# A two-layer mixer kernel on one Trainium2 core: how x is loaded at the start, and where the two filter networks stand

## The chip, the cores and the metric

The kernel runs on one core of one Trainium2 chip. The core has five engines with a queue of instructions each: TensorE (PE) for matmuls, VectorE (DVE), ScalarE (ACT), GpSimd (POOL) and SyncE (SP), which here only starts DMA transfers. Each engine takes its instructions in the order in which they were laid out when the program was built, and waits on semaphores for what it needs. The metric is the device time of one execution in microseconds (us); the median of several runs is the result.

## The reference, cut to what matters

x (512 tokens, 1024 wide) and a context (256 tokens) go through two layers. In each layer a modulation row is computed from c, the normalised x is projected by w_in, and three mixers (differential attention, grouped attention, and a long convolution named hyena) make y, which w_out projects. The convolution's filter comes from a small network of three sine layers, once for length 512 and, in the first layer, once for length 256:

```python
def _hyena_filter(L, w1, b1, w2, b2, w3, b3, w4, freq):
    ...
    h = jnp.sin(fr * (z @ w1.astype(f32) + b1.astype(f32)))
    h = jnp.sin(fr * (h @ w2.astype(f32) + b2.astype(f32)))
    h = jnp.sin(fr * (h @ w3.astype(f32) + b3.astype(f32)))
    h = h @ w4.astype(f32)
    ...
def reference(...):
    for l in range(DEPTH):
        shift, scale, gate = jnp.split(jax.nn.silu(c) @ ada_w[l] + ada_b[l], 3, axis=-1)
        h = _rms(x, norm_g[l]) * (1.0 + scale[:, None]) + shift[:, None]
        hc = _rms(xc, norm_g[l]) * (1.0 + scale_c) + shift_c
        qa, ka, va, ga, qg, kg, vg, gg, uh, gh = _prep(h @ w_in[l], gq_q_g[l], gq_k_g[l])
        ...
        filt = _hyena_filter(L, hy_w1[l], ...)
        y = _mixer_output(...)
        if update_ctx:
            filt_c = _hyena_filter(Lc, hy_w1[l], ...)
            ...
        x = x + gate[:, None] * y
    return _rms(x, final_g)
```

## The kernel before, in words

All products are made in three passes: a float32 value is split into a high part (wh, uh, made by a cast on ACT, L152) and the rest (wl, ul, a subtraction on DVE, L156), and `mm3` issues high x high (L138), high x low (L139) and low x high (L140). A weight tile raw [128, 1024] comes in by a DMA on SP (L528) and is split into wh and wl; eight such buffers go round.

The program begins with `startup_loads`. SP loads c, x in four tiles, and between these the small constants: the networks' inputs and weights, identity, columns. An x tile holds 256 of the 1024 columns of all 512 tokens, so that each row read is 1 KB. `x0_rms` sums the squares on ACT, in pieces of 256 columns (L497), and `rsqrt_cols` makes the inverse root r with Ln and Exp on ACT (L168, L169) and a Newton step on DVE (L171 to L175). `scale_x` multiplies x by r on ACT and DVE (L510, L512).

Then follows a loop over four quarters of the width. In each, `mod_quarter` multiplies the modulation weights (adaw tiles, DMA at L357) with silu(c) in 32 small matmuls (psm, L365), adds the bias (mrow, L368), transposes (pst, L370) and writes the columns mA and mB (L372, L373). `make_hT_x` transposes two chunks of x on PE (L467), applies mA and mB on ACT (hf, L469) and splits the result on DVE (hT, L457 and L458). `start_proj` then gives these two chunks to the first two hyena projections (xv of b = 0 and 1, 96 matmuls of 128x512 in all over the four quarters). Next the context is done in the same way (cq, L481, L486; 96 matmuls of 128x256). The results are filtered by a short convolution (cv, L684 to L687) and multiplied on POOL (ux, uc, L707).

The two networks are `filter_mlp`. For each of the three layers PE makes one product (L217 for the first, L219 after it), DVE computes the argument and reduces it to the sine's range in six operations (v and m, L222 to L228), and ACT takes the sine (hmlp, L231). The network for 512 has tiles of 128x512, that for 256 of 64x256; both write their products into the PSUM tile S0. The sine needs another table of functions on ACT than the rest of the kernel; the set in use is changed by an ACT_TABLE_LOAD. In the kernel before, the first network is written ahead of the loop over the quarters and the second within its first turn. A table load (guard) in the second turn brings back the set that holds Exp, and the context's load and all that is written later is kept behind guard by `tc.issue_after`.

`mlp_stack` splits the networks' outputs (hst). `filter_gen` then multiplies them by the last weights (psh, L280 and L281), applies the decay on DVE (fw L284, bw L288), forms the sum s on POOL (L299) and the difference on DVE (L300), sums squares (q on ACT, accf on POOL, L294), splits s and the difference (uh, ul), and transforms them by products with tables (EOf, L308 to L310). PSUM tiles come from small pools: S has two buffers (S0 and S1 at the start, later EOf), pj two, T and O one each. After the filter's transform the next projections (xg) begin.

A scheduler decides, when the program is built, in what order the instructions stand in each engine's queue; it goes by the written order, by its own estimate of times, and by the pools.

Of the kernel before, what the change touches and what calls it, by code (L numbers as in the profile page):

```python
# [10 lines left out]
F32 = mybir.dt.float32  # L11
F32R = mybir.dt.float32r
AF = mybir.ActivationFunctionType
# [55 lines left out]
def hybrid_mixer(ctx: ExitStack, tc: tile.TileContext, a, out):  # L69
# [94 lines left out]
    def rsqrt_cols(ms, n, scale, pool=None):  # L164
        m = small(n, pool)
        DVE.tensor_scalar(out=m, in0=ms, scalar1=scale, scalar2=EPS, op0=ALU.mult, op1=ALU.add)
        r = small(n, pool)
        ACT.activation(r, m, AF.Ln)  # L168
        last_exp[0] = ACT.activation(r, r, AF.Exp, scale=-0.5)  # L169
        t = small(n, pool)  # L170
        DVE.tensor_tensor(out=t, in0=r, in1=r, op=ALU.mult)  # L171
        DVE.tensor_tensor(out=t, in0=t, in1=m, op=ALU.mult)
        DVE.tensor_scalar(out=t, in0=t, scalar1=-0.5, scalar2=1.5, op0=ALU.mult, op1=ALU.add)
        r2 = small(n, pool)
        DVE.tensor_tensor(out=r2, in0=r, in1=t, op=ALU.mult)  # L175
        return r2
# [14 lines left out]
    def startup_loads(xd):  # L191
        zt = [up.tile([33, n], F32, tag="u", name="zt") for n in (512, 256)]
        ws = [ta.tile([128, 64] if i else [33, 2, 64], F32, tag="ta", name="wf") for i in range(3)]
        bc = cp.tile([128, 4], F32, tag="bc", name="bc")
        ct = sw.tile([128, 16], F32, tag="sw", name="ct")
        few = [[(ct, a["cT"]), (zt[0], a["z512"]), (ws[0], a["hy_w1"])], [(bc, a["hy_b"]), (ws[1], a["hy_w2"])],
               [(zt[1], a["z256"]), (ws[2], a["hy_w3"])], [(ident, a["ident"]), (cols[0], a["cols"][0])]]
        xq = []
        for q in range(4):
            t = pa.tile([128, 4, 256], F32, tag="pa", name="xq")  # L200
            SP.dma_start(t, xd[:, q * 256:(q + 1) * 256].rearrange("(t p) n -> p t n", p=128))
            xq.append(t)
            for dst, src in few[q]:
                SP.dma_start(dst, src)
        return ct, xq, (zt, ws, bc)
# [255 lines left out]
    def make_hT_x(xblk, A, B, ks, pools):  # L461
        res = []
        for k in ks:
            pool, tag = pools[k % len(pools)]
            ps = pool.tile([128, 512], F32, tag=tag, name="pst")
            for t in range(4):
                PE.transpose(ps[:, t * 128:(t + 1) * 128], xblk(k, t), ident)  # L467
            h = tp.tile([128, 512], F32, tag="tp", name="hf")
            ACT.activation(h, ps, AF.Identity, bias=B[:, k, 0:1], scale=A[:, k, 0:1])  # L469
            res.append(split2(h, [512]))  # L470
        return res
# [19 lines left out]
    def row_sums(s, t, n):  # L491
        r = small(t)
        DVE.tensor_reduce(out=r, in_=s[:, :t * n].rearrange("p (t q) -> p t q", q=n), axis=AX.X, op=ALU.add)
        return r

    def sumsq(dst, src, eng_tile):
        ACT.activation(eng_tile, src, AF.Square, accum_out=dst)  # L497

    def x0_rms(xq):
        sx = sw.tile([128, 16], F32, tag="sw", name="sx")  # L500
        for q, t in enumerate(xq):
            for i in range(4):
                sumsq(sx[:, 4 * i + q:4 * i + q + 1], t[:, i], ta.tile([128, 256], F32, tag="ta", name="sqj"))
        return rsqrt_cols(row_sums(sx, 4, 4), 4, 1.0 / D)

    def scale_x(xq, r):
        for q, x in enumerate(xq):
            for t in range(x.shape[1]):
                if q % 2:
                    ACT.activation(x[:, t], x[:, t], AF.Copy, scale=r[:, t:t + 1])  # L510
                else:
                    DVE.tensor_scalar(out=x[:, t], in0=x[:, t], scalar1=r[:, t:t + 1], scalar2=None, op0=ALU.mult)  # L512

    def load_c0(cd):
        cq = []
        sc = sw.tile([128, 16], F32, tag="sw", name="sc")
        for q in range(2):
            t = pa.tile([128, 2, 512], F32, tag="pa", name="cq")
            SP.dma_start(t, cd[:, q * 512:(q + 1) * 512].rearrange("(t p) n -> p t n", p=128))
            for i in range(2):  # L520
                sumsq(sc[:, 2 * i + q:2 * i + q + 1], t[:, i], pt.tile([128, 512], F32, tag="pt", name="sqj"))
            cq.append(t)
        scale_x(cq, rsqrt_cols(row_sums(sc, 2, 2), 2, 1.0 / D))
        return cq
# [747 lines left out]
    first_weights(0, 0)  # L1272
    ada = [ada_load(0)]
    first_weights(1, 0)
    scale_x(xq, rx)
    S0 = pS.tile([128, 1024], F32, tag="S", name="psf")
    fb = cp.tile([128, 4], F32, tag="fb", name="fb")
    for i in range(3):
        DVE.tensor_tensor(out=fb[:, i:i + 1], in0=mlp[2][:, i:i + 1], in1=mlp[2][:, 3:4], op=ALU.mult)
    ada.append(ada_load(1))  # L1280
    hl = [filter_mlp(0, *mlp, fb, S0, last_exp[0].ins)]
    acc = [[pj.tile([128, 512], F32, tag="pj", name="psf") for _ in range(2)]]
    S1 = pS.tile([128, 2, 512], F32, tag="S", name="psf")
    acc.append([S1[:, i] for i in range(2)])
# [2 lines left out]
    def start_proj(q):  # L1287
        for b in range(2):
            for mb in range(2):
                for k in (2 * q, 2 * q + 1):  # L1290
                    Wh, Wl = W0[b][k // 4]
                    mm3(acc[b][mb], Wh[:, k % 4, mb * 128:mb * 128 + 128], Wl[:, k % 4, mb * 128:mb * 128 + 128],
                        hx[k][0], hx[k][1], k == 0, k == 7)

    for q in range(4):
        mod_quarter(q, cs, ada[q], rows, *mods[0])
        hx += make_hT_x(lambda k, t: xq[k // 2][:, t, (k % 2) * 128:(k % 2) * 128 + 128], *mods[0], (2 * q, 2 * q + 1),
                        ((pT, "T"),))
        if q == 0:
            ada.append(ada_load(2))  # L1300
            first_weights(0, 1)
            first_weights(1, 1)
            hl.append(filter_mlp(1, *mlp, fb, S0, last_exp[0].ins))
        elif q == 1:
            ada.append(ada_load(3))
            ctx.enter_context(tc.issue_after(last_ada[0].ins))
            with tc.issue_after(hl[0][1].ins), tc.issue_after(hl[1][1].ins):
                guard = ACT.preload_act_table_set(ACT_SET)
        elif q == 2:
            with tc.issue_after(guard.ins):  # L1310
                cq = load_c0(a["ctx"])
        else:
            hc = []
            hc_gen = make_hT_c(hc, cq, *mods[0], 0)
            for _ in range(4):
                next(hc_gen)
            SP.dma_start(cols[1], a["cols"][1])
            w4 = w4_load(0)
            gate = last_lo[0].ins
        if q > 0:  # L1320
            start_proj(q - 1)
    start_proj(3)
    h = {"0x": mlp_stack(hl[0][0], 0, 512), "0c": mlp_stack(hl[1][0], 0, 256)}
    SP.dma_start(hst1[:, :], mlp_stack(hl[0][0], 1, 512).bitcast(F32))
    ctx.enter_context(tc.issue_after(guard.ins))
    f0 = filter_gen(0, "0x", 512, h, w4)
    with tc.issue_after(gate):
        next(f0)
# [170 lines left out]
```

## Time and profile before

| | us |
|---|---|
| median of 3 runs | 1585.81 |
| lowest and highest run | 1583.59, 1588.69 |
| the profiled execution's own time | 1585.86 |
| its span in the trace | 1584.1 |

| engine | busy us | share of the span |
|---|---|---|
| PE | 1500.6 | 95% |
| DVE | 1128.4 | 71% |
| ACT | 828.7 | 52% |
| POOL | 404.5 | 26% |

The profile is of one execution, taken by the hardware profiler. An engine is busy while it executes; the time in which it waits on a semaphore is idle. PEld is the loading of weights into TensorE, which overlaps with its matmuls. PEclk is the clock that TensorE was granted, as a share of full speed. A timeline row gives the start, the duration, the engine with the line of the code, the operation, its output and inputs, and, in square brackets, how long the engine was idle just before it and what ended this wait. The span starts a little after the execution's own time does, so the two differ by 1.8 us.

### The profile page before, as it was taken

How to read it: one execution, taken by the hardware profiler on the slowest of the kernel's cores; microseconds unless marked ns; L12 is line 12 of the kernel's file. 1: busy time of each engine (PE TensorE's matmuls, PEld its weight loads, DVE VectorE, ACT ScalarE, POOL GpSimd, SP SyncE). 2: the span in 40 equal slices, each digit the busy share in tenths (PEclk: the TensorE clock that was granted, in tenths of full speed). 3: DMA queues.
4: the chain of work that ended last, by engine and by line, in shares of the span. 5: the costliest groups of instructions: out<-in, count | busy, mean ns of one | idle time of the engine just before them, and what ended most of it. 6: DMA issues, size and time to landing. Idle time of an engine off the chain costs nothing. (4 is left out here: it accounts for less than half of the span.)

```text
span 1584.1 us, 27024 instructions
## 1 busy us (share of the span) xinstructions
PE 1500.6 (95%) x10166; PEld 1349.7 (85%) x10166; DVE 1128.4 (71%) x2168; ACT 828.7 (52%) x1611; POOL 404.5 (26%) x436
## 2 busy tenths in 40 slices
PE   5989999999999999998999999998999999898997
PEld 3768888999998989898888878888999998798885
DVE  6767777877767475877754588769887656768657
ACT  5544343555466465666653356324556555657633
POOL 0243433212222141212002124233322223214014
PEclk9999999999999999999999999999999999999999
DMA  9437666323425253315343444764422222116242
GB/s 347 140 121 252 213 206 202 121 88 110 150 94 158 94 157 121 114 48 183 117 141 132 137 142 154 244 210 143 139 64 88 87 97 87 57 48 209 60 157 80
DMA packets 102134, 218.30 MB, mean 138 GB/s; under 512 B 11377, under 2 KB 46131, under 8 KB 102004
## 3 DMA queue, kind: packets, MB, share of 16 engines
q1 hardware_dynamic: 91492, 180.14, 34.6%
q0 software_dynamic: 9936, 35.39, 7.2%
q8 instruction: 80, 1.31, 0.3%
q10 hardware_dynamic: 576, 1.05, 0.2%
q14 instruction: 50, 0.41, 0.1%
HBM read 176.02 MB, written 40.52 MB: 137 GB/s over the span
## 5 line engine op out<-in xcount | busy, mean ns | idle before, releaser
L138 PE MATMUL psf<-hT,wh 128*128 128x512 f32 (+1 forms) x768 | 269.4, 355 | 13.5 <-DVE kL L1045 7.2
L138 PE MATMUL pst<-wh,hT 128*128 128x256 f32 x960 | 275.7, 287 | 6.7 <-DVE t L602 6.3
L140 PE MATMUL pst<-wh,hT 128*128 128x256 f32 x960 | 274.9, 286 | 0.0
L139 PE MATMUL pst<-wl,hT 128*128 128x256 f32 x960 | 274.4, 286 | 0.0
L139 PE MATMUL psf<-hT,wh 128*128 128x512 f32 (+1 forms) x768 | 268.3, 350 | 0.0
L140 PE MATMUL psf<-hT,wl 128*128 128x512 f32 (+1 forms) x768 | 267.6, 349 | 0.0
L156 DVE TENSOR_TENSOR wl<-raw,wh 128x1024 fp32r<-128x1024 f32 x140 | 178.2, 1274 | 93.2 <-ACT wh L152 82.9
L152 ACT ACTIVATE wh<-raw 128x1024 fp32r<-128x1024 f32 x140 | 147.9, 1057 | 94.5 <-PE psf L139 42.9
L138 PEld LDWEIGHTS pst<-wh,hT 128*128 128x128 f32 x960 | 184.4, 192 | 12.7 <-issue 10.0
L637 ACT ACTIVATE P<-S,sa 128x768 f32<-128x768 f32 (+1 forms) x160 | 130.2, 814 | 111.8 <-DVE sa L634 63.5
L139 PEld LDWEIGHTS pst<-wl,hT 128*128 128x128 f32 x960 | 184.5, 192 | 1.2 <-issue 0.8
L140 PEld LDWEIGHTS pst<-wh,hT 128*128 128x128 f32 x960 | 184.6, 192 | 0.9 <-issue 0.8
L138 PEld LDWEIGHTS psf<-hT,wh 128*128 128x128 f32 x768 | 146.2, 191 | 34.9 <-ACT P L977 4.3
L139 PEld LDWEIGHTS psf<-hT,wh 128*128 128x128 f32 x768 | 146.8, 191 | 16.7 <-issue 0.4
L140 PEld LDWEIGHTS psf<-hT,wl 128*128 128x128 f32 x768 | 146.4, 191 | 16.9
L634 DVE TENSOR_REDUCE sa<-S 128x1 f32<-128x768 f32 (+1 forms) x160 | 134.6, 841 | 26.9 <-PE S L629 17.7
L582 DVE TENSOR_TENSOR pl<-T,ph 128x512 fp32r<-128x512 f32 x156 | 107.0, 686 | 43.2 <-ACT ph L581 40.5
L581 ACT ACTIVATE ph<-T 128x512 fp32r<-128x512 f32 x156 | 92.6, 593 | 74.9 <-PE T L648 74.0
L138 PE MATMUL px<-wh,yT 128*128 128x512 f32 x320 | 126.1, 399 | 4.8 <-ACT P L977 3.6
L139 PE MATMUL px<-wl,yT 128*128 128x512 f32 x320 | 126.2, 395 | 0.0
L140 PE MATMUL px<-wh,yT 128*128 128x512 f32 x320 | 125.9, 394 | 0.0
L892 POOL TENSOR_TENSOR P<-P,sa 128x768 f32<-128x768 f32 (+1 forms) x40 | 52.4, 1309 | 207.6 <-DVE sa L639 198.1
(301 smaller groups left out, 3410.1 us busy)
## 6 DMA issues: line engine op xcount, KB each, us to landing
raw<-in_w_in SPq DMA_DIRECT2D x104, 512.0 KB, 4.1
raw<-in_w_out SPq DMA_DIRECT2D x36, 512.0 KB, 3.9
adaw<-in_ada_w SPq DMA_DIRECT2D x32, 512.0 KB, 4.6
tab<-in_inv POOLq DMA_DIRECT2D x20, 512.0 KB, 4.7
tab<-in_fwd POOLq DMA_DIRECT2D x18, 512.0 KB, 4.8
adaw<-in_ada SPq DMA_DIRECT2D x16, 512.0 KB, 10.6
yT<-yx POOLq DMA_DIRECT2D x16, 512.0 KB, 6.9
gl<-gd SPq DMA_DIRECT2D x60, 128.0 KB, 2.4
```

Of the source, the lines that this page charges most:

```text
L138: i0 = PE.matmul(ps, sh, mh, start=first, stop=False)
L139: PE.matmul(ps, sh, ml, start=False, stop=False)
L140: return i0, PE.matmul(ps, sl, mh, start=False, stop=last)
L152: ACT.activation(hi, src, AF.Copy)
L156: last_lo[0] = e.tensor_tensor(out=lo, in0=src, in1=hi.bitcast(F32), op=ALU.subtract)
L581: ACT.activation(dh, ps, AF.Copy)
L582: return DVE.tensor_tensor(out=dl, in0=ps, in1=dh.bitcast(F32), op=ALU.subtract)
L634: DVE.tensor_reduce(out=nm, in_=S[:, :n], axis=AX.X, op=ALU.max, negate=True)
L637: ACT.activation(P[:, :n], S[:, :n], AF.Exp, bias=nm, accum_out=s)
L892: POOL.tensor_tensor(out=P[:, :n], in0=P[:, :n], in1=rs.to_broadcast([128, n]), op=ALU.mult)
```

## The change

x is loaded in four tiles of 128 tokens with all 1024 columns, so that each row read is 4 KB. The squares are summed in four operations of 1024 columns, whose scratch output comes from another pool, and the four sums need no adding up. The new `scale_rows` multiplies halves of 512 columns, even tiles on DVE and odd ones on ACT. The transposes read the new layout.

Both networks are now written behind the last `start_proj`, one after the other, and the table load that brings back Exp behind them. The context's load and the work that is written later no longer wait for it.

```diff
-            t = pa.tile([128, 4, 256], F32, tag="pa", name="xq")
-            SP.dma_start(t, xd[:, q * 256:(q + 1) * 256].rearrange("(t p) n -> p t n", p=128))
+            t = pa.tile([128, 1024], F32, tag="pa", name="xq")
+            SP.dma_start(t, xd[q * 128:(q + 1) * 128, :])
...
     def x0_rms(xq):
         sx = sw.tile([128, 16], F32, tag="sw", name="sx")
-        for q, t in enumerate(xq):
-            for i in range(4):
-                sumsq(sx[:, 4 * i + q:4 * i + q + 1], t[:, i], ta.tile([128, 256], F32, tag="ta", name="sqj"))
-        return rsqrt_cols(row_sums(sx, 4, 4), 4, 1.0 / D)
+        for i, t in enumerate(xq):
+            sumsq(sx[:, i:i + 1], t, dt.tile([128, 1024], F32, tag="dt", name="sqj"))
+        return rsqrt_cols(sx[:, 0:4], 4, 1.0 / D)
+
+    def scale_rows(xq, r):
+        for h in range(2):
+            for t, x in enumerate(xq):
+                v = x[:, h * 512:(h + 1) * 512]
+                if t % 2:
+                    ACT.activation(v, v, AF.Copy, scale=r[:, t:t + 1])
+                else:
+                    DVE.tensor_scalar(out=v, in0=v, scalar1=r[:, t:t + 1], scalar2=None, op0=ALU.mult)
...
-    scale_x(xq, rx)
+    scale_rows(xq, rx)
...
-    hl = [filter_mlp(0, *mlp, fb, S0, last_exp[0].ins)]
...
-        hx += make_hT_x(lambda k, t: xq[k // 2][:, t, (k % 2) * 128:(k % 2) * 128 + 128], *mods[0], (2 * q, 2 * q + 1),
+        hx += make_hT_x(lambda k, t: xq[t][:, k * 128:(k + 1) * 128], *mods[0], (2 * q, 2 * q + 1),
...
-            hl.append(filter_mlp(1, *mlp, fb, S0, last_exp[0].ins))
...
-            with tc.issue_after(hl[0][1].ins), tc.issue_after(hl[1][1].ins):
-                guard = ACT.preload_act_table_set(ACT_SET)
         elif q == 2:
-            with tc.issue_after(guard.ins):
-                cq = load_c0(a["ctx"])
+            cq = load_c0(a["ctx"])
...
     start_proj(3)
+    hl = [filter_mlp(sp, *mlp, fb, S0, last_exp[0].ins) for sp in range(2)]
+    with tc.issue_after(hl[0][1].ins), tc.issue_after(hl[1][1].ins):
+        ACT.preload_act_table_set(ACT_SET)
...
-    ctx.enter_context(tc.issue_after(guard.ins))
```

In the order of the built program the change shows at these places. A row has the line, the operation, output and inputs, and the output's shape. On PE, in the front, the kernel before has this from the first quarter's modulation to the first x projection (psf from hT):

```order
L365 MATMUL psm<-adaw,cs 32x128 x16
L219 MATMUL psf<-hmlp,wf 64x512 x2
L365 MATMUL psm<-adaw,cs 32x128
L467 MATMUL pst<-ident,xq 128x128 x4
L365 MATMUL psm<-adaw,cs 32x128 x14
L217 MATMUL psf<-zt,wf 64x256
L365 MATMUL psm<-adaw,cs 32x128
L138 MATMUL psf<-hT,wh 128x512
```

and the changed kernel has this:

```order
L370 MATMUL pst<-ident,mrow 128x98
L365 MATMUL psm<-adaw,cs 32x128 x8
L467 MATMUL pst<-ident,xq 128x128 x4
L138 MATMUL psf<-hT,wh 128x512 x3
L217 MATMUL psf<-zt,wf 64x512 x2
L365 MATMUL psm<-adaw,cs 32x128 x8
L139 MATMUL psf<-hT,wh 128x512
```

The products of the networks' later layers (L219) are gone from here, the first product of the 512 network (L217) stands behind three matmuls of a projection, and the x projections begin among the second quarter's modulation.

On PE, at the end of the context projections (the last psf of 128x256), the kernel before has:

```order
L309 MATMUL EOf<-ul,tab 128x512
L310 MATMUL EOf<-uh,tab 128x512
L138 MATMUL psf<-hT,wh 128x256
L139 MATMUL psf<-hT,wh 128x256
L140 MATMUL psf<-hT,wl 128x256
L280 MATMUL psh<-uh,hst 128x512
L281 MATMUL psh<-ul,hst 128x512
```

and the changed kernel:

```order
L138 MATMUL psf<-hT,wh 128x256
L139 MATMUL psf<-hT,wh 128x256
L140 MATMUL psf<-hT,wl 128x256
L219 MATMUL psf<-hmlp,wf 64x256 x2
L280 MATMUL psh<-uh,hst 128x512
L281 MATMUL psh<-ul,hst 128x512
```

The filter's products and part of its transform (psh, EOf) stood among the context projections; now they follow them, and two products of the 256 network stand between.

On DVE the six operations of a layer of the 256 network stand in the kernel before between the last step for the 512 network and the second quarter's modulation columns:

```order
L228 TENSOR_SCALAR v<-v 128x512
L222 TENSOR_SCALAR v<-psf,bc,fb 64x256
L224 TENSOR_SCALAR m<-v 64x256
L225 TENSOR_SCALAR m<-m 64x256
L226 SCALAR_TENSOR_TENSOR v<-m,v 64x256
L227 SCALAR_TENSOR_TENSOR v<-m,v 64x256
L228 TENSOR_SCALAR v<-v 64x256
L372 COPY mB<-pst 128x4
```

In the changed kernel they stand behind the splits of the weights of the projections to come:

```order
L228 TENSOR_SCALAR v<-v 128x512
L156 TENSOR_TENSOR wl<-raw,wh 128x1024
L222 TENSOR_SCALAR v<-psf,bc,fb 64x256
L224 TENSOR_SCALAR m<-v 64x256
L225 TENSOR_SCALAR m<-m 64x256
L226 SCALAR_TENSOR_TENSOR v<-m,v 64x256
L227 SCALAR_TENSOR_TENSOR v<-m,v 64x256
L228 TENSOR_SCALAR v<-v 64x256
L222 TENSOR_SCALAR v<-psf,bc,fb 64x256
```

The three layers of the 256 network now follow one another on DVE with nothing between them, and the filter's operands (hst, fw, bw) come behind all three.

## Rows read from the trace of the kernel before

**Rows 1.** Windows: stretch, length, busy PE PEld DVE ACT POOL, PEclk, DMA share, GB/s

```profile
5.00:10.00 5.00, 1.97 (x4) 0.32 (x4) 2.58 (x9) 4.33 (x22) 0.00 (x0) 1.00 0.97 302
20.00:25.00 5.00, 3.53 (x69) 2.31 (x68) 3.89 (x9) 2.29 (x4) 0.00 (x0) 1.00 1.01 410
40.04:62.60 22.56, 22.56 (x160) 17.37 (x161) 15.10 (x46) 13.77 (x30) 4.79 (x5) 1.00 0.33 101
62.60:81.60 19.00, 17.19 (x124) 15.39 (x123) 17.67 (x28) 11.56 (x20) 5.64 (x4) 1.00 0.57 187
86.00:88.00 2.00, 1.91 (x5) 1.52 (x6) 2.00 (x4) 0.00 (x0) 0.00 (x0) 0.55 0.00 0
114.00:1584.00 1470.00, 1410.98 (x9531) 1283.44 (x9529) 1048.81 (x2005) 767.55 (x1481) 376.12 (x408) 0.99 0.41 133
```

**Rows 2.** Timeline of PE: last x projection, last context matmul, first xg projection

```profile
62.37 0.40 PE L140 MATMUL psf<-hT,wl 128*128 128x512 f32 x1
...
81.34 0.28 PE L140 MATMUL psf<-hT,wl 128*128 128x256 f32 x1
...
90.78 0.39 PE L138 MATMUL psf<-hT,wh 128*128 128x512 f32 x1
```

**Rows 3.** Timeline of PE: products of the networks in the front

```profile
25.17 1.08 PE L219 MATMUL psf<-hmlp,wf 64*64 64x512 f32 x4
...
28.09 0.64 PE L217 MATMUL psf<-zt,wf 33*64 33x256 f32 x2
...
36.60 0.64 PE L219 MATMUL psf<-hmlp,wf 64*64 64x256 f32 x2 [1.25 <-ACT hmlp L231]
...
43.38 0.64 PE L219 MATMUL psf<-hmlp,wf 64*64 64x256 f32 x2
```

**Rows 4.** Timeline of ACT, then DVE: a weight split, the table load, a sine

```profile
13.50 1.06 ACT L152 ACTIVATE wh<-raw 128x1024 fp32r<-128x1024 f32 x1 [0.42 <-DMA raw<-in_w_in]
...
14.91 1.28 ACT L231 ACT_TABLE_LOAD   x1
16.20 0.63 ACT L231 ACTIVATE hmlp<-v 128x512 f32<-128x512 f32 x1
...
14.59 1.23 DVE L156 TENSOR_TENSOR wl<-raw,wh 128x1024 fp32r<-128x1024 f32 x1 [1.10 <-ACT wh L152]
```

**Rows 5.** Timeline of DVE, then ACT: first and last step of a network layer

```profile
7.97 0.81 DVE L222 TENSOR_SCALAR v<-psf,bc,fb 128x512 f32<-128x512 f32 x1 [0.19 <-PE psf L217]
...
11.19 0.43 DVE L228 TENSOR_SCALAR v<-v 128x512 f32<-128x512 f32 x1
...
33.70 0.53 DVE L222 TENSOR_SCALAR v<-psf,bc,fb 64x256 f32<-64x256 f32 x1
...
35.81 0.28 DVE L228 TENSOR_SCALAR v<-v 64x256 f32<-64x256 f32 x1
...
36.13 0.42 ACT L231 ACTIVATE hmlp<-v 64x256 f32<-64x256 f32 x1 [1.68 <-DVE v L228]
```

**Rows 6.** Timeline of DVE, then POOL: steps of the filter and of the short convolution

```profile
70.06 0.69 DVE L284 TENSOR_TENSOR fw<-psh,dc 128x512 f32<-128x512 f32 x1 [0.54 <-PE psh L281]
...
80.08 0.73 DVE L687 SCALAR_TENSOR_TENSOR cv<-psf,cols,cv 128x511 f32<-128x511 f32 x1
...
72.57 1.28 POOL L299 TENSOR_TENSOR s<-fw,bw 128x512 f32<-128x512 f32 x1 [10.55 <-DVE bw L288]
...
75.34 1.36 POOL L294 TENSOR_TENSOR accf<-q,q 128x512 f32<-128x512 f32 x1 [1.48 <-ACT q L292]
76.67 1.74 POOL L707 TENSOR_TENSOR ux<-cv 128x512 f32<-128x512 f32 x1
```

**Rows 7.** Waits of PE, 114 to 300: us in total, times, longest

```profile
PE pst L138 <- DVE t L602: 3.4, 1, 3.4
PE yps L138 <- DMA tab<-in_inv: 1.8, 1, 1.8
...
PE EO L138 <- DMA tab<-in_fwd: 1.3, 1, 1.3
```

## The prediction

> **What bounds the kernel now.** I read the busy time by stretch first. From 114 us to the end PE works 1410.98 of 1470 us [rows 1], and the engines that feed it have room there: this part is a queue of matmuls, whose length the change leaves alone. What the change touches ends at the first xg projection, at 90.78 [rows 2]. Before that point three stages follow each other. In the front (to the last x projection, 62.37 [rows 2]) PE waits for modulation weights while the DMA queues are full (share 1.01 at 410 GB/s between 20 and 25 us), and from 40.04 to 62.60 it is full itself (22.56 of 22.56). In the context stage (62.6 to 81.6) DVE is the fuller engine, 17.67 of 19 us against 17.19 for PE [rows 1]. In the filter stage, from the last context matmul at 81.34 to 90.78 [rows 2], PE waits for the chain DVE, POOL, ACT that makes the filter's operands, and runs part of it at 0.55 of its clock [rows 1]. So I sum at one point, the start of the first xg projection: the same PE instructions lie before it in both kernels, and behind it the order is the same but for swaps. A shift there is a shift of the end, unless something gives it back.
>
> **The front: taken −5 us, bounds −9 and −2.** The x tiles are 2.10 MB. While x is read, the queues move 302 GB/s at share 0.97; later, with 4 KB rows, 410 GB/s at share 1.01 [rows 1]. So 6.9 us become 5.1: at most −1.8 us for x and for all streams queued behind it on SP. Nothing, if it is the small loads between them that hold the rate down.
>
> The networks' instructions leave the front. On PE, the last L219 pair of the 512 network (1.08), two L219 of the 256 network (0.64 each), one L217 (0.64), and the wait of 1.25 us in front of the L219 at 36.60, which is a wait for a sine [rows 3]. Against that the L217 of the 512 network, formerly done early, stands between the first projections; I give it the 1.08 of the L219 with the same shape. That is 1.08 + 2 x 0.64 + 0.64 + 1.25 − 1.08 = 3.2 us less on a PE that is otherwise full. Together −5.0.
>
> The row sums of x come earlier too: Ln and Exp no longer stand behind a weight split (wh 1.06, wl 1.23) [rows 4], and 16 short squares become four long ones. DVE loses the networks' chains there (below). I count nothing for it: PE is covered by its own queue once the first projections run. If instead the start of the projections follows these, and the psm matmuls of the next quarter no longer stand ahead of them, another 4 us can go: the end −9. If the streams do not move, and PE waits for the first hT where it used to do the networks, −2 is left.
>
> **The context stage: taken +1.5, bounds −1 and +4.** Here the 512 network's chains stand now, each 7.97 to 11.62 = 3.65 us on DVE [rows 5]; two and a half of them fall in this stage: 9.5 us. What leaves it is the filter's first half: some ten operations of the size of fw (0.69 [rows 6]): 6.9 us. DVE goes from 17.67 to 20.3 us in a stage of 19: with DVE full, +1.3, and +1.5 with its handovers. The lower end is a DVE that keeps the stage at 19 and a PE that has a few psh and EOf less to do; the upper one counts the first two sines in full as waits of PE (its own work here falls to some 15 us, so most is covered by projections).
>
> **From the last context matmul to the first xg projection: taken +20, bounds +16 and +22.** Before, this takes 90.78 − 81.34 = 9.44 us, because the filter's first half was done within the context stage. After the change nothing of the filter can begin until the networks have ended, and the 256 network ends last: on PE both its L219 stand behind the last context matmul, and on DVE its first operation stands behind two weight splits, of which the second has to wait for the buffer that the last context matmul reads. From that matmul on, in series:
>
> - the last split: wh 1.06 on ACT and wl 1.23 on DVE [rows 4], with handovers 2.5 us;
> - three 64x256 chains on DVE, 33.70 to 36.09 = 2.39 each [rows 5]: 7.2; three sines of 0.42 [rows 5] with handovers, 0.5 each: 1.5; two L219 of 0.64 [rows 3] with handover: 1.4; the table load that brings back the Exp set, 1.28 [rows 4]; the stack of two halves, two operations of the size of fw, 1.3. Sum 12.7;
> - L219 at half clock after such idling: +0.6 (row 86 to 88 shows 0.55 after PE had stood [rows 1]);
> - the filter's first part as at 70: psh about 1.1 at half clock, fw and bw 0.69 each, s on POOL 1.28, accf 1.36 and ux 1.74 behind it [rows 6]. ux frees a buffer of cv, the cv steps (three at up to 0.73 [rows 6]) free the PSUM tile S1, and that is the bank of the second set of EOf. That is 9.0; the EOf and psh left then, fourteen, of which five take 2 us at half clock [rows 1] and the other nine an estimated 0.3 each: 4.7. Sum 13.7.
>
> 2.5 + 12.7 + 0.6 + 13.7 = 29.5 us in place of 9.44: +20. Lower end: the last split done before the last context matmul, and a second filter half that needs no half clock (11.3 in place of 13.7): +16. Upper end: every one of some ten handovers 0.2 longer: +22. What could hide all this is the projection xg, which has no need of the filter; but on PE it stands behind the EOf, and an engine takes its instructions in order.
>
> A table switch is in this chain once more than in the old one, where it lay under x. The row shows a load of 1.28 us at 14.91 and the sine at 16.20, 0.01 us behind it [rows 4]. The Trainium skill ("ScalarE: Activation LUTs", What ACT_TABLE_LOAD costs) gives 1.283 us for the load and 1.38 for a drain, 2.66 together for each switch; by it the sum would be an estimated 1.4 us longer. On load the trace agrees, a drain ahead of the sine it does not show, so the row decides.
>
> **The sum.** −5 + 1.5 + 20 = +16.5 on the profiled execution's 1585.86 us: 1602.4, so 1602. That execution is 0.05 us from the median of the three runs (1585.81; 1583.59 to 1588.69), so nothing is to be moved. With all terms at one end: −9 − 1 + 16 = +6, or −2 + 4 + 22 = +24.
>
> **Rivals.** First, the other side: the delay is **given back later**, and the time is not slower. PE stands 59 of the 1470 us behind 114 [rows 1]. If these waits are for things with a pace of their own (loads, POOL's tables), a later start takes them away. Between 114 and 300 the largest is for DVE (t, 3.4 us), then tables for 1.8 and 1.3 [rows 7]. Against it: t is made from PE's own matmuls, so it comes later as PE does; only the two tables are paced by a queue, 3.1 us. With those, 1599. For the time to count as no change, 11.7 of the 16.5 us would have to come back; at all of them, 1586. If the front and the context stage are also at their lower ends, −9 and −1, it is faster: 6.5 less, 1579. For: transfers ahead of use run on while PE waits, and could pull later waits in as well.
>
> Second, **the half clock spreads.** In the context stage PE gets small waits in place of one stretch of work. If it is there at 0.55 for the time that it shows after an idle stretch [rows 1], some 7 us of matmuls take twice as long where they are not covered by DVE: +6, so 1608. For: PE has some 4 us less work in a stage that DVE now ends. Against: at 17.19 of 19 us the clock was 1.00 [rows 1].
>
> Third, **it doesn't do what it says:** the 256 network finds gaps and runs under the context projections, so that only the table load and the filter's first part stand exposed, +8 in place of +20: 1590. Against: PE's order puts its L219 behind the last context matmul, and this order is fixed before the run. I give it next to nothing, with other causes.
>
> **How the numbers follow.** Forecast 0.72 (1592 to 1610); half clock 0.12; given back 0.12; the third and all else 0.04. The likeliest gives 1602. A difference of 0.3%, 4.8 us, is about what a measurement of this kernel can tell from no change. The forecast and the half clock are slower, with half of the rest: 0.86. Of the delay given back 0.09 is within 0.3%, with the other half of the rest 0.11; 0.03 is faster. The range 1591 to 1610 takes in the forecast and most of the half clock (0.72 and about 0.1); what lies under it is the delay given back.
>
> **What would show it.** In the changed kernel: the last x projection some 5 us earlier than before (near 57); the last context matmul near 78; then three 64x256 chains in a row on DVE with PE idle, about 12 us, a table load, and POOL's s, accf and ux with PE idle again; the first xg projection near 107. From there on every row about 16 us later to the end. Wrong would be: a sine of 64x256 before the last context matmul; a front that ends past 60 (the x load gains nothing) or before 53; or a shift that shrinks between 114 and 300, which is the first rival.

## The result, and the profile after

The changed kernel takes 1609.44 us (median of 5 runs, 1608.44 to 1611.93) beside 1587.34 for the kernel before (5 runs): a ratio of 1.0139, 95% interval 1.0124 to 1.0154, or 22.1 us more. The prediction was 1602, in a range from 1591 to 1610. The time lies just inside the upper end of the range. The direction and the main cause were right; two terms of the sum were not: the front gave less than I took, and the filter stage cost more. A third term, the context stage, came out near its size, but not for the reason given. The profiled execution took 1611.59 us, its span is 1609.8.

Busy times of the changed kernel (part 1 of its page): PE has 6 us more for the same number of recorded matmuls (10166 in both), and the windows below show stretches in which it ran at a lower clock.

```profile
PE 1506.9 (94%) x10166; PEld 1353.0 (84%) x10166; DVE 1123.5 (70%) x2163; ACT 826.7 (51%) x1583; POOL 407.0 (25%) x436
```

The points of the sum in its PE timeline, against [rows 2]: the last x projection at 61.55 (before 62.37), the last context matmul at 81.44 (81.34), the first xg projection at 113.69 (90.78).

```profile
61.55 0.39 PE L140 MATMUL psf<-hT,wl 128*128 128x512 f32 x1
...
81.44 0.28 PE L140 MATMUL psf<-hT,wl 128*128 128x256 f32 x1
...
113.69 0.39 PE L138 MATMUL psf<-hT,wh 128*128 128x512 f32 x1
```

So of the 22.9 us that the common point moved, the front gave back 0.8, the context stage took 0.9 more, and the stretch from the last context matmul to xg took 32.25 in place of 9.44, 22.8 more. The windows, to be read like [rows 1]: in the 16.3 us from 81.5 to 97.8 PE works 2.44, and after that it works through the filter's products at 0.67 of its clock.

```profile
20.00:25.00 5.00, 3.47 (x26) 2.08 (x28) 3.77 (x8) 2.50 (x3) 0.00 (x0) 0.79 1.01 406
25.00:30.00 5.00, 5.00 (x40) 2.25 (x40) 0.90 (x2) 1.64 (x2) 0.00 (x0) 0.53 1.01 408
81.50:97.80 16.30, 2.44 (x6) 0.58 (x6) 9.87 (x23) 5.66 (x9) 0.00 (x0) 0.59 0.20 65
97.80:113.70 15.90, 12.61 (x33) 8.81 (x34) 13.96 (x18) 6.28 (x11) 8.31 (x6) 0.67 0.23 66
```

PE's own timeline of this stretch shows the three waits: for the sine before each L219 of the 256 network, and for the split of the operands (hst) before the first psh. The last column is the idle time just before and what ended it.

```profile
86.79 1.11 PE L219 MATMUL psf<-hmlp,wf 64*64 64x256 f32 x2 [5.08 <-ACT hmlp L231]
90.96 1.11 PE L219 MATMUL psf<-hmlp,wf 64*64 64x256 f32 x2 [3.06 <-ACT hmlp L231]
97.82 0.76 PE L280 MATMUL psh<-uh,hst 128*128 128x512 f32 x1 [5.75 <-DVE hst L238]
```

Behind xg the shift stays: pn (L327), at 113.95 in the kernel before, stands at 136.37 in this one, 22.4 later. The last matmul of yps (L140) ahead of 300 us, at 296.48 in the kernel before, stands at 318.07, 21.6 later, and the spans differ by 25.7.

### The profile page after: what moved, and what is told of

Same layout as the page of the kernel before. It is cut to its first block, busy times and chain, and to the rows that moved or that the text cites. A ratio compares the mean times of both kernels' runs of the same rounds, so it can differ in the third digit from the quotient of the medians.

```text
span 1609.8 us, 27015 instructions
## 1 busy us (share of the span) xinstructions
PE 1506.9 (94%) x10166; PEld 1353.0 (84%) x10166; DVE 1123.5 (70%) x2163; ACT 826.7 (51%) x1583; POOL 407.0 (25%) x436
## 5 line engine op out<-in xcount | busy, mean ns | idle before, releaser
L140 PE MATMUL pst<-wh,hT 128*128 128x256 f32 x960 | 274.7, 286 | 0.0
L140 PE MATMUL psf<-hT,wl 128*128 128x512 f32 (+1 forms) x768 | 268.6, 350 | 0.0
L140 PEld LDWEIGHTS pst<-wh,hT 128*128 128x128 f32 x960 | 184.6, 192 | 1.7 <-issue 1.7
L140 PEld LDWEIGHTS psf<-hT,wl 128*128 128x128 f32 x768 | 147.1, 191 | 17.8 <-issue 0.8
L642 DVE TENSOR_REDUCE sa<-S 128x1 f32<-128x768 f32 (+1 forms) x160 | 134.6, 841 | 28.7 <-PE S L637 22.9
L140 PE MATMUL px<-wh,yT 128*128 128x512 f32 x320 | 126.3, 396 | 0.0
```

Source lines behind the costliest of these rows:

```text
L140: return i0, PE.matmul(ps, sl, mh, start=False, stop=last)
L642: DVE.tensor_reduce(out=nm, in_=S[:, :n], axis=AX.X, op=ALU.max, negate=True)
```

## The experiments

Each kernel was timed beside runs of the kernel before on the same chip. "Time" is the ratio to these; in us it is that ratio less 1, times 1588. The four stage points are starts in the profiled execution. "mrow" is the first quarter's addition on DVE (L368), from which the first columns mA and mB are made. "clock" is PE's mean granted clock from 20 to 30 us in the profiled execution.

| kernel | mrow | clock | last x | last context | first xg | ratio (95%) | us |
|---|---|---|---|---|---|---|---|
| before | 23.14 | 1.00 | 62.37 | 81.34 | 90.78 | 1 | 0 |
| changed | 20.00 | 0.66 | 61.55 | 81.44 | 113.69 | 1.0139 (1.0124, 1.0154) | +22 |
| e1_tiles | 20.10 | 1.00 | 58.18 | 79.15 | 86.50 | 0.9965 (0.9950, 0.9980) | −6 |
| e2_nets | 20.10 | 0.83 | 58.93 | 77.68 | 113.38 | 1.0162 (1.0141, 1.0184) | +26 |
| e3_turns | 19.53 | 0.83 | 60.25 | 78.45 | 106.04 | 1.0064 (1.0043, 1.0084) | +10 |
| e4_no256 | 20.15 | 1.00 | 58.59 | 78.18 | 98.91 | 1.0085 (1.0065, 1.0106) | +13 |
| e5_late_r | 24.12 | 0.83 | 64.97 | 88.72 | 95.92 | 1.0044 (1.0027, 1.0061) | +7 |
| e6_early_r | 24.64 | 1.00 | 63.65 | 90.07 | 98.78 | 1.0025 (1.0012, 1.0039) | +4 |
| e7_warm | 20.08 | 0.83 | 60.03 | 79.91 | 124.84 | 1.0217 (1.0200, 1.0235) | +34 |
| e8_mrow_first | 22.71 | 0.83 | 63.36 | 90.90 | 98.00 | 1.0067 (1.0049, 1.0086) | +11 |
| e9_mrow_late | 22.96 | 0.83 | 62.70 | 84.34 | 93.09 | 1.0035 (1.0024, 1.0047) | +6 |
| e10_noacc | 20.00 | 0.83 | 60.17 | 80.06 | 110.11 | 1.0111 (1.0090, 1.0132) | +18 |

### e1_tiles and e2_nets: the two halves of the change

e1_tiles has the new load and `scale_rows`, with the networks where the kernel before has them:

```diff
     ada.append(ada_load(1))
+    hl = [filter_mlp(0, *mlp, fb, S0, last_exp[0].ins)]
...
             first_weights(1, 1)
+            hl.append(filter_mlp(1, *mlp, fb, S0, last_exp[0].ins))
...
-    hl = [filter_mlp(sp, *mlp, fb, S0, last_exp[0].ins) for sp in range(2)]
```

and likewise, not shown here, guard and the two waits on it. e2_nets is the reverse: x in tiles of [128, 4, 256], 16 squares and `scale_x`, the networks behind the last x projection.

> Only the x part of the change (token tiles, four long squares, scale_rows); both networks, the table load and the waits on it stand where the kernel before has them. In the changed kernel the last x projection came only 0.8 us earlier, not 5. Theory A: the 4 KB rows buy next to nothing, because SP issues the first weight tile at 9.62 (before 9.55), so the streams behind x don't move: the last x projection within 1 us of 62.37 and the time within 2 us of the kernel before. Rival B: the x tiles do buy some 2 to 4 us at the front, and moving the networks took it away again: last x projection at 58.5 to 60.5, the time 2 to 4 us under the kernel before.

> Only the networks are moved (behind the last x projection, table load behind them, no waits on it); x is loaded and scaled as before. Theory A: the whole loss is here, the first xg projection at 113 to 115 as in the changed kernel (113.69), the time 22 us over the kernel before, within 2 us of the changed kernel. Rival B (the x tiles buy 2 to 4 us): 2 to 4 us slower than the changed kernel, 24 to 26 us over the kernel before.

Theory A fell, and the gain is larger than rival B had it. The x part alone is worth some 6 us (interval 3 to 8): it is faster than both kernels of this study. The last x projection is at 58.18, and the first xg projection 4.3 us earlier than before. e2_nets is 26 us over the kernel before, 4 more than the changed kernel (interval about 0 to 8); its stage points do not show these 4 us, since its first xg projection stands where the changed kernel has it (113.38, 113.69). So the two halves have opposite signs. What carried the gain I did not know yet: in e1_tiles SP issues the first weight tile at 9.24 us (before 9.55), so the streams did not move much.

### e4_no256 and e3_turns: what fills the gap

e4_no256 leaves the 256 network out (the 512 network's output takes its place), e3_turns, shown here, writes both layer by layer:

```diff
-        return o, sin
+            yield o, sin
...
-    hl = [filter_mlp(sp, *mlp, fb, S0, last_exp[0].ins) for sp in range(2)]
+    nets = [filter_mlp(sp, *mlp, fb, S0, last_exp[0].ins) for sp in range(2)]
+    for _ in range(3):
+        hl = [next(net) for net in nets]
```

> The changed kernel without the 256 network (left out: its three layers; the 512 network's output takes its place, so the second filter is another one). Theory: PE idles from the last context matmul (81.44) because the 256 network's three rounds (DVE chain, sine, L219) run there alone, from 83.9 to 95.0 us. Without them the filter's operands are split at about 86 in place of 97, the first xg projection comes near 103, and the time is 10 to 11 us under the changed kernel, 11 to 12 over the kernel before. Rival: the filter's start is held by something else as well (loads of decay and last weights, POOL): then 4 us or less is won.

> The changed kernel with the two networks written layer by layer in turns (512, 256, 512, 256, ...) in place of one after the other. Two rounds of both then lie under the context projections; behind the last context matmul one round of each is left: a 128x512 chain of 3.65 and a 64x256 chain of 2.39 in place of three of 2.39. Theory (the tail is the length of the serial chain left there): hst about 3 us earlier than 97, the time 2 to 4 us under the changed kernel, 18 to 20 over the kernel before. Rival (the tail is set by the number of rounds of one network, since DVE has room): two rounds of 4 us less, 8 us won.

In e4_no256 the first psh follows the last context matmul after 4.9 us (78.18, 83.07) in place of 16.4 (81.44, 97.82): 11.5 us of the gap are the 256 network's three rounds, as expected. The time is 0.0054 of ratio under the changed kernel, 8.6 us, a little less than the 10 to 11 expected; the intervals allow both. Its PE timeline:

```profile
78.18 0.28 PE L140 MATMUL psf<-hT,wl 128*128 128x256 f32 x1
83.07 0.77 PE L280 MATMUL psh<-uh,hst 128*128 128x512 f32 x1 [4.61 <-DVE hst L238]
...
98.91 0.39 PE L138 MATMUL psf<-hT,wh 128*128 128x512 f32 x1
```

In e3_turns this stretch is 11.75 us (78.45, 90.20), 4.6 less than in the changed kernel, against 3 expected by the theory and 8 by the rival. The theory is the nearer one. In the changed kernel a round that stands alone takes 4.0 to 4.2 us (83.90, 87.94, 92.11), not the 2.4 of its chain on DVE: for 1.7 us of each DVE waits for the sine and the next L219. In e3_turns the two chains left follow each other on DVE without a gap (80.88 to 86.88), so each network's sine and product lie beside the other's chain. xg stands 7.7 us earlier than in the changed kernel, since the context stage and the front were shorter too; the time fell by 12 (interval about 8 to 16).

From the first psh to xg it is 15.87, 15.86, 15.84 and 15.84 us in the changed kernel, e2, e3 and e4. My sum had 13.7. So this term was too small by 2.2 us, and the same in all four. Two experiments are on it.

### e7_warm and e10_noacc: why the filter stage takes 15.9 us

e7_warm adds matmuls that nobody reads, to keep PE busy in the gap:

```diff
+    def extra(n, w, o):
+        for _ in range(n):
+            PE.matmul(S0[64:128, 512:768], w[0:64], o[0:64, 0:256], start=True, stop=True)
...
                         PE.matmul(eps[kb][:, f], th, sd[f][0], start=(t == 0), stop=False)
+                        if key == "0x" and tt == 0 and kb == 0 and f == 0:
+                            for _ in range(8):
+                                PE.matmul(eps[0][:, 1], th, sd[0][0], start=True, stop=True)
```

> The changed kernel with matmuls added that nobody reads, in the places where PE stands idle behind the last context matmul: 5, 5 and 10 of 64x256 among the 256 network's products, 8 of 128x512 after the filter's first EOf; all other instructions keep their order on PE and DVE. In the changed kernel the L219 there took 1.11 in place of 0.64, and from 105.47 to 111.2 the EOf and psh stand 0.43 apart in place of 0.23, at PEclk 0.50. Theory: the half clock is a price of its own, some 4 us of the 32.25 between the last context matmul and the first xg projection: with PE busy the clock stays at 1.00, that stretch is 28 to 29 us, and the time 3 to 4 us under the changed kernel (about 18 over the kernel before). Rival: the operands (s, ul, cv) set the pace of the EOf, and the clock costs nothing: under 1 us.

The first part went wrong: the added matmuls write the PSUM tile of which DVE reads v, so that DVE's next chain waited for all of them (6.64 and 9.40 us), and the gap grew to 29 us. Nor did the clock rise: between 85 and 90 us PE was busy all the time with these small products, at 0.50 (the columns here: stretch, length, busy PE, PEclk, DMA share, GB/s).

```profile
85.00:90.00 5.00, 5.00 (x15) 0.50 0.19 75
```

The second part answers the question. Behind the eight matmuls of 128x512 (114.42 to 117.75) the EOf stand 0.23 apart, not 0.43, and the stretch from the first psh (108.98) to xg (124.84) is still 15.86 us: PE caught up and then waited for ul.

```profile
123.35 0.50 PE L323 MATMUL EOf<-ul,tab 128*128 128x512 f32 x1 [1.31 <-DVE ul L156]
```

A full clock buys nothing there, so something other than PE sets this stretch.

e10_noacc leaves out POOL's first sums of squares and nothing else:

```diff
-                if tt == 0:
+                if key == "0x" and tt < 2:
+                    pass
+                elif tt == (2 if key == "0x" else 0):
                     POOL.tensor_tensor(out=acc, in0=q1, in1=q2, op=ALU.add)
```

> The changed kernel without POOL's sums of squares of the filter's first two parts (left out: accf of the first two of four row blocks, so the filter is normalised by half of its sum); PE and DVE have the same order. In the changed kernel, e2, e3, e4 and e7 the stretch from the first psh to the first xg projection is 15.84 to 15.87 us, whatever the clock, so a chain of operations sets it; in it the DVE operations that run beside POOL's accf and ux take 1.75 in place of 0.69 (L300 at 101.99, ul at 103.66, ul at 110.35). Theory: POOL's work is in the chain twice, in its own time and in DVE's: without accf the stretch shrinks by 2 to 3.5 us (12.4 to 13.9) and the time by as much, to 18.5 to 20 over the kernel before. Rival: the stretch is set by the transfers or by PE (table tiles, PSUM banks): 15.3 or more.

The stretch is 13.66 us (96.45, 110.11), 2.2 less, and the time 4 us under the changed kernel (interval about 0 to 9). Four timelines follow: DVE in the changed kernel, POOL in the changed kernel, and DVE and POOL in e10_noacc.

```profile
101.99 1.75 DVE L300 TENSOR_TENSOR fw<-fw,bw 128x512 f32<-128x512 f32 x1 [1.39 <-POOL s L299]
103.66 1.75 DVE L156 TENSOR_TENSOR ul<-s,uh 128x512 fp32r<-128x512 f32 x1
105.34 0.68 DVE L156 TENSOR_TENSOR ul<-fw,uh 128x512 fp32r<-128x512 f32 x1
...
108.96 1.46 DVE L300 TENSOR_TENSOR fw<-fw,bw 128x512 f32<-128x512 f32 x1
110.35 1.77 DVE L156 TENSOR_TENSOR ul<-s,uh 128x512 fp32r<-128x512 f32 x1
```

```profile
100.68 1.27 POOL L299 TENSOR_TENSOR s<-fw,bw 128x512 f32<-128x512 f32 x1 [41.83 <-DVE bw L288]
101.92 1.27 POOL L294 TENSOR_TENSOR accf<-q,q 128x512 f32<-128x512 f32 x1
103.15 1.71 POOL L715 TENSOR_TENSOR ux<-cv 128x512 f32<-128x512 f32 x1
```

```profile
100.61 1.75 DVE L302 TENSOR_TENSOR fw<-fw,bw 128x512 f32<-128x512 f32 x1 [1.39 <-POOL s L301]
102.28 0.68 DVE L156 TENSOR_TENSOR ul<-s,uh 128x512 fp32r<-128x512 f32 x1
103.06 0.69 DVE L156 TENSOR_TENSOR ul<-fw,uh 128x512 fp32r<-128x512 f32 x1
```

```profile
100.55 1.26 POOL L717 TENSOR_TENSOR ux<-cv 128x512 f32<-128x512 f32 x1
```

A DVE operation on two tiles in SBUF takes 0.68 us here when POOL is idle. When it starts during one of POOL's here, it ends 0.55 us behind that one, as all 17 such operations of the filter in the changed kernel do: accf ends at 103.19 and L300 at 103.74, ux at 104.86 and ul at 105.41. So the price of a meeting is what is left of POOL's operation, here 0.8 to 1.1 us more for DVE. POOL waits in the same way: ux takes 1.71 where it starts during L300 and 1.26 in e10_noacc, where it starts first. L302, which there starts beside ux, is still long. An operation that reads one of its inputs from PSUM is not held: the cv at 107.91 took 0.75 beside s (107.36 to 108.65), and those at 61.38 and 62.37, with POOL idle, took 0.74 and 0.75. The Trainium skill ("SBUF — State Buffer", Who interferes with whom) says that a DVE instruction with two SBUF inputs contends with a GpSimd instruction that reads SBUF, and that the port pair they share is an exclusive lock; the trace agrees, with the ends just given.

DVE's queue meets POOL's four times in this stretch of the changed kernel: at 101.99 and 103.66, and in the filter's second part at 108.96 and 110.35 beside q and accf. That is 4.0 us of waiting on DVE; without POOL's sums three of the four go, and the second ul of s ends 2.8 us earlier in its stretch. The stretch itself falls by only 2.2, since PE's own queue then sets it: in e10_noacc PE works from 103.02 to 110.11 without a wait.

### e5_late_r, e6_early_r, e8_mrow_first, e9_mrow_late: where the front's gain comes from

e5_late_r puts r behind the first weight split in e1_tiles; e6_early_r keeps that split behind r in the kernel before.

```diff
-        return rsqrt_cols(sx[:, 0:4], 4, 1.0 / D)
+        return sx[:, 0:4]
...
     first_weights(0, 0)
+    with tc.issue_after(last_lo[0].ins):
+        rx = rsqrt_cols(rx, 4, 1.0 / D)
```

```diff
-    first_weights(0, 0)
+    raw0 = rp.tile([128, 4, 256], F32, tag="raw", name="raw")
+    SP.dma_start(raw0, a["w_in"][0, xv[0], :, 0:4])
+    with tc.issue_after(last_exp[0].ins):
+        W0[0].append(split(wp, "w", raw0, "act", "dve"))
```

> e1_tiles (token tiles, networks in the old place) with one wait put back: Ln and Exp of the row sums stand behind the first weight split (wh on ACT, wl on DVE), as they do in the kernel before. In e1_tiles r was ready at 13.2 us in place of 16.5, and the last x projection came at 58.2 in place of 62.4. Theory A (the early r makes the gain, the 4 KB rows themselves none): r at 16 to 16.5 again, the last x projection at 60.5 to 62.5, the time within 2 us of the kernel before. Rival B (the load's 4 KB rows and the fewer squares make it): the last x projection stays under 59.5 and the time 4 to 5 us under the kernel before.

> The kernel before, with one thing changed: the first weight split (wh, wl) is kept behind the Exp of the row sums; x is loaded in 1 KB rows as before. Theory A: r comes at about 14.3 in place of 16.5, the last x projection 1 to 2.5 us earlier than 62.4, the time 1 to 3 us under the kernel before. Rival B: nothing moves, the last x projection within 0.5 of 62.4 and the time within 1 us.

e5_late_r lost the whole gain and more (+7 us; its profiled execution lies 8.6 us under its median, so only the order of its stages is used). That would speak for r. But e6_early_r had r ready at 14.9 in place of 16.5 and came out later at the front, 63.65, and 4 us slower. Theory A fell again. In its DVE queue mrow stood behind the second weight split, whose tile lands near 20 us (e6_early_r, timeline of DVE):

```profile
22.90 1.22 DVE L156 TENSOR_TENSOR wl<-raw,wh 128x1024 fp32r<-128x1024 f32 x1
24.04 0.68 DVE L227 SCALAR_TENSOR_TENSOR v<-m,v 128x512 f32<-128x512 f32 x1
24.64 0.28 DVE L368 TENSOR_TENSOR mrow<-psm,mrow 128x128 f32<-128x128 f32 x1
```

So I formed a third theory: the front starts when DVE comes to mrow. e8 moves that split behind mrow in the kernel before, e9 moves mrow behind that split in e1_tiles, where everything else stays early.

```diff
-    first_weights(1, 0)
+    raw1 = rp.tile([128, 4, 256], F32, tag="raw", name="raw")
+    SP.dma_start(raw1, a["w_in"][0, xv[1], :, 0:4])
...
         mod_quarter(q, cs, ada[q], rows, *mods[0])
+        if q == 0:
+            with tc.issue_after(add[0].ins):
+                W0[1].append(split(wp, "w", raw1, "act", "dve"))
```

```diff
+        with ExitStack() as late:
+            if q == 0:
+                late.enter_context(tc.issue_after(lo1[0]))
+            DVE.tensor_tensor(out=rq, in0=ps, in1=rq, op=ALU.add)
...
     first_weights(1, 0)
+    lo1[0] = last_lo[0].ins
```

> The kernel before with one order changed on DVE: the second weight split (wl of the second weight tile, which lands near 20 us) is kept behind the first quarter's mrow addition. e6_early_r had r 1.6 us earlier and yet a later front, because on DVE mrow stood behind that wl (22.90), at 24.64. Theory C (the front starts when DVE comes to mrow; mrow needs the psm matmuls, which stand on PE behind the products of the 512 network and the transposes of scaled x, and it needs a DVE queue in which the second wl doesn't stand ahead): here the psm matmuls still end at 22.4, so only wl's part goes: mrow at 22.4 to 22.7 in place of 23.14, the last x projection 0.5 to 1.2 us earlier than 62.4, the time 0 to 1.5 us under the kernel before. Rival D (mrow's place in the queue is of no account): 62.4 and no change.

> e1_tiles (token tiles, networks in the old place; mrow at 20.10, last x projection 58.18) with one order changed on DVE: the first mrow addition is kept behind the second weight split. r, the sines and the squares are as early as in e1_tiles. Theory C: mrow at 23 us, the last x projection 2 to 3.5 us later (60.2 to 61.7), and the time 2 to 4 us over e1_tiles: most of the gain is gone though x is loaded and scaled as early. Rival D: the last x projection stays within 0.7 of 58.2 and the time at 0.9965 of the kernel before.

e9_mrow_late bears theory C out in its direction. r, squares and scaling are as early (r at 13.3), mrow is at 22.96, and the last x projection moves from 58.18 to 62.70, the first xg projection from 86.50 to 93.09, the time from 6 us under the kernel before to 6 over. mrow accounts for 2.9 of the 4.5 us that the last x projection moved; the order on PE changed too, and its clock was 0.83 in place of 1.00, so the rest cannot be put down to mrow. Its DVE timeline:

```profile
21.82 1.23 DVE L156 TENSOR_TENSOR wl<-raw,wh 128x1024 fp32r<-128x1024 f32 x1 [1.64 <-ACT wh L152]
22.96 0.28 DVE L372 TENSOR_TENSOR mrow<-psm,mrow 128x128 f32<-128x128 f32 x1
```

In e1_tiles' DVE timeline mrow stands ahead of that split:

```profile
20.10 0.29 DVE L368 TENSOR_TENSOR mrow<-psm,mrow 128x128 f32<-128x128 f32 x1
```

Both conditions are needed: the psm matmuls must be done, and DVE must not be held by the split. In eight of the twelve kernels mrow starts 0.1 us behind the last psm matmul ahead of it; in the other four (before, e5, e6, e9) the split stands between, and it is 0.8 to 3.2. With the new load an early r brings the psm early: they end at 19.98 in e1_tiles and at 22.94 in e5_late_r. But it is not the only way. e2_nets has x in 1 KB rows and r at 16.3, as in the kernel before, but no network layer ahead on PE and DVE, and its mrow is as early as in e1_tiles:

```profile
16.32 2.19 DVE L521 TENSOR_SCALAR xq<-xq,sm 128x256 f32<-128x256 f32 x8
...
20.10 0.29 DVE L368 TENSOR_TENSOR mrow<-psm,mrow 128x128 f32<-128x128 f32 x1 [1.59 <-issue]
```

The second influence on the front is PE's clock. The changed kernel, e4, e7 and e10 have the same PE order up to the last x projection and mrow within 0.15 us; that projection starts at 61.55 with the clock at 0.66, at 60.03 and 60.17 with 0.83, and at 58.59 with 1.00. A step of 0.17 is thus worth 1.5 us.

e8 shows the other side. There the psm still end at 22.6, mrow gains only 0.4 us (22.71), as theory C had it; but the last x projection came a microsecond later, where theory C had it 0.5 to 1.2 earlier, and the time was 11 us over the kernel before. The clock in 20 to 30 us was 0.83 in place of 1.00; at 1.5 us for that, an estimate from the four kernels above, the front would have come out 0.5 earlier. Most of the 11 us is elsewhere: its context stage is 27.5 us long (63.36 to 90.90), as it is in e6 (26.4) and e5 (23.8), against 19.0 before. Each of these small edits made the scheduler lay out the context stage anew, with waits of 2.4 us for the filter's operands in the middle of it, as this row of e8's PE timeline:

```profile
82.33 0.36 PE L138 MATMUL psf<-hT,wh 128*128 128x256 f32 x1 [2.39 <-ACT uh L152]
```

The times of e5, e6 and e8 are thus no measure of r or mrow alone; their stage points in the front are nearer to one, read together with the clock. Which of the scheduler's rules makes the new layout was not tried.

## Why the prediction was right or wrong

**The exposed chain: right, and the reason for the sign.** The 256 network's sines all came behind the last context matmul, the first at 86.32. The gap from the last context matmul to the first psh was predicted as 2.5 + 12.7 + 0.6 = 15.8 us and is 16.4. Its parts: the last split 2.5 (81.44 to 83.90), three rounds 11.1 (83.90 to 95.02; 10.1 and the half clock's 0.6 in the sum), the table load 1.28, the stack 1.5. e4_no256 took 11.5 us of it away with the network. The end of it in the changed kernel's ACT timeline:

```profile
94.60 0.42 ACT L231 ACTIVATE hmlp<-v 64x256 f32<-64x256 f32 x1 [3.69 <-DVE v L228]
95.04 1.28 ACT L1328 ACT_TABLE_LOAD   x1
96.33 1.59 ACT L237 ACTIVATE hst<-hmlp 64x512 fp32r<-64x512 f32 x3
```

The table load starts 0.02 behind the sine and the next operation 0.01 behind the load: no drain of 1.4 us, as weighed by [rows 4].

**The filter's first part: mis-sized, 13.7 in place of 15.9.** The step that failed is the chain "fw and bw, s, accf, ux, cv", with accf and ux as links of POOL's own. What sets the stretch is DVE's queue, which POOL's operations hold up four times, 0.8 to 1.1 us each; for DVE the sum had the durations that its operations have alone. The kernel before already held such a meeting: the ux of 1.74 in [rows 6] takes 1.26 where it starts first. With POOL's sums gone the stretch is 13.66; that this is the sum's number is chance, since the sum had accf in it. The half clock, to which the sum gave a part of this stretch, costs nothing in it (e7_warm).

**The front: −5 predicted, −0.8 measured, and for the wrong reasons.** The prediction named a front that ends past 60 as a sign of being wrong, and it ended at 61.55. In this step three things were wrong. The −1.8 us from the 4 KB rows did not come: between 5 and 10 us the load moved 324 GB/s where it moved 302 (410 only later, [rows 1]), and SP issued the first weight tile at 9.62 as before (9.55), so no stream behind x started earlier. The networks' leaving was taken as 3.2 us less work on a full PE; what it gave is an earlier start, mrow at 20.00 in place of 23.14. Either half of the change alone brings this, e1_tiles by the new load with its earlier r, to which I gave nothing, and e2_nets without it; so the two do not add up. And in the changed kernel's profiled execution PE ran at 0.79 and 0.53 between 20 and 30 us, where the kernel before and e1_tiles show 1.00. e4_no256 has the same PE order in the front and 1.00 there, and its last x projection is at 58.59, 3.0 earlier. So without the clock the front gives −3.8, near the −5, 3.0 of it by mrow.

**The context stage: the size near (+0.9, taken as +1.5), the reason not.** The sum took DVE as full there, with 20.3 us of work in a stage of 19. The networks' chains came and the filter's first half left, but DVE's work fell, from 17.67 in [rows 1] to 16.42 in the same window of the changed kernel:

```profile
62.60:81.60 19.00, 15.99 (x114) 13.18 (x114) 16.42 (x29) 10.04 (x15) 0.00 (x0) 1.00 0.26 83
```

Two of the 512 network's chains fell into it, not two and a half. From the last x projection to the last context matmul PE works 16.66 us, before 17.16, and stands idle for 3.2 in place of 1.8: it waits 1.4 for hT, 1.1 for hf and 0.6 for a sine. That the sizes agree is luck.

**The rivals.** Given back later: no. The table has the shift of the first xg projection and the shift of the time for eleven kernels; they differ by −5 to +5 us (e3 +15.3 and +10; e4 +8.1 and +13) with no leaning to a smaller time at a larger shift, and the changed kernel has +22.9 and +22. The sign named for it, a shift that shrinks between 114 and 300, shows 0.8 us (22.4 to 21.6) of the 3.1 that the two tables could give. Half clock spreading: it did come, but in the front (3 us), while the context stage ran at 1.00; the place I gave it was wrong, its price about half of what I gave. That the 256 network finds gaps under the context projections: no, in the changed kernel; e3_turns shows how much of it can.

The measured 22.1 us lie inside the bounds of the sum (+6 to +24), near the upper end: the front's term was 4.2 too good, the filter's 2.2 too small, the gap's 0.6, and the context's 0.6 too large. The lower bound of +16 for the gap and the filter comes out at +15 from its own two numbers (2.5 for the split, 2.4 for the clock), and the sum's at +5; nothing hangs on it.

## What to carry to other kernels

A step moved "behind" something lands on the critical path as soon as no other work stands behind it in each engine's own queue: read the tail from the built order, engine by engine, and add up its serial chain. Two changes bundled in one can have opposite signs; here the load alone is 6 us faster than the kernel before, and the move costs some 26. A chain put together from single durations is too short where DVE and POOL work side by side on tiles in SBUF: add, for a DVE operation that starts during one of POOL's, what is left of that one.

## What the runs showed of the hardware

- A DVE operation with two inputs in SBUF that started during a POOL tensor operation (accf, q, ux) ended 0.55 us behind it: 0.68 us became 1.46 to 1.77. One with an input in PSUM did not wait (cv, 0.75 beside s).
- PE's granted clock was 0.50 from 85 to 90 us in e7_warm, while PE was busy with 64x256 products all the time (5.00 of 5), and 1.00 from 120 us on, behind the eight 128x512 matmuls of 114.4 to 117.8. In the front the clock differed between kernels of the same PE order (0.53 in the changed kernel from 25 to 30 us, 1.00 in e4_no256 and 0.95 in e7_warm); what decides between them was not tried.
- x in 1 KB and in 4 KB rows came in at 302 and 324 GB/s; between them small loads take part of the time, so this is no measure of the row size alone.
